# Residual held token-major: projections that end in it keep the activations stationary

## The chip, the cores and the metric

The program runs on one core of a Trainium2 chip. The metric is the device time of one execution in microseconds (us). An engine is named as the profile names it: PE is TensorE (its matmuls; PEld its weight loads), DVE is VectorE, ACT is ScalarE, POOL is GpSimd and SP is the engine that issues most DMAs. Each works through its own instructions in order and waits for the others through semaphores.

## The reference

Two layers are applied to x of 256 tokens by 2048 features, all in float32. Cut to what matters here:

```python
# first block
h = rms_norm(x, norm_mix_g)
proj = h @ w_in                                   # attention, recurrence, short convolution, gates
x = x + (g_a * y_a + g_b * y_b + g_c * y_c) @ w_out
h = rms_norm(x, norm_mlp_g)
x = x + jnp.square(jax.nn.relu(h @ w_mlp_up)) @ w_mlp_down      # 2048 -> 8192 -> 2048
x = rms_norm(x, final_g)
# second block
h = rmsnorm(x, g_mix_2) @ w_in_2                  # state space branch, sparse attention
x = x + jnp.concatenate([y_ssd, y_att], axis=-1) @ w_out_2
u = rmsnorm(x, g_mlp_2) @ w_up_2
return x + jnp.square(jax.nn.relu(u)) @ w_down_2
```

rms_norm(x, g) is x / sqrt(mean over features of x squared + 1e-6) * g. The x that goes from line to line is the residual.

## The kernel before, in words

**Jobs.** All large products are jobs of 512 output columns of a weight matrix. A job walks over the 2048 (or 1024) inputs in steps of 256, that is two blocks k of 128. For a step SP loads 256 x 512 weights into a tile `raw`; ACT rounds them to `hi` (a float32r value) and DVE computes the rest `lo = raw - hi`. Activations are split in the same way into an `Operand` of 16 blocks, each with a high and a low half of 256 tokens. A product is hi*hi + hi*lo + lo*hi, accumulated in PSUM (`products`).

**Two forms of a job.** Where the weights are stationary, each 128x128 piece of `hi` is loaded into PE and the 512 columns "high and low half" of the operand stream past it; each piece of `lo` sees the 256 columns of the high half. The output has features on the partitions and tokens along the row, its two partial sums side by side; `total` adds them (an ACT copy `cr`, a DVE add `tot`). A job has two outputs of 256 features, q = 0 and 1, each of two PSUM banks. In the other form, `tok=True`, 128 tokens of the operand are stationary and 512 columns of weights stream past them: hi*hi, hi*lo and lo*hi are each a matmul of 512 columns into the same place, and the output has tokens on the partitions. Before, this form serves for the values v of both attentions and for the last down-projection (f = 3 of the second block), whose result is stored to memory as it is.

**Residual.** `self.res` is four tiles, features on the partitions. `load_x` turns x with PE (`xT`), copies it by DVE to `xf` and writes that to memory as `xs`; the output projection loads it back. `residual` is the evacuation of jobs that end in the residual. It adds the job's result (in the down-projections scaled by a row `rrow`), and at the last addition it also makes the next operand (`split_scaled`) and sums squares over features (`squares`). `norm` in `output` and `between` fold these sums, reduce them over partitions with PE (`mean`), take the inverse square root in small DVE steps (`rsqrt`), and spread a column over a row with PE (`row`). `next_res` scales the residual for the second block and writes it to `xs`. `turn_res` turns the residual back (32 transposes, in the last up-projection) for the last jobs.

**What sets the order.** `stream` writes the instructions of all engines in program order; each engine then runs its own in that order. For each step it issues the loads 7 steps ahead, the split of weights 5 steps ahead, then the step's matmuls. Behind them `side.tick` lets short work of the branches (lanes) go on where a cost model says its inputs are ready, and `advance` takes each pending evacuation one `yield` further. At a job's last step its evacuation begins at once. Weight-stationary jobs do q = 0 of their first two steps before q = 1 of either. The output projection of the second block is cut in two halves over its inputs, so that it can begin while attention still runs.

**Jobs in order.** First block: 28 jobs of `w_in` with three branches between them, then the output projection (4 jobs, operand `mixop`), then for f = 0 to 3 four up-projections (operand `hm`) and four down-projections (operand `hid`, by `relu2`). Second block: jobs of `w_in_2` (operand `h`, side lanes beside them), the output projection in 8 halves (operand `ymix`), and again f = 0 to 3.

All instructions have line 104 in the profile, which is the helper that records them, so they are told apart by their tiles. Tiles are slots of 128 x 1024 float32, 43 in number, shared by weights, operands and residual.

Of the kernel before, what the change touches and what calls it, by code (L numbers as in the profile page):

```python
# [19 lines left out]
P = 128  # L20
T = 256
# [153 lines left out]
class Builder:  # L175
# [188 lines left out]

    def fold(self, acc):
        self.nc.vector.tensor_tensor(acc[:, 0, :], acc[:, 0, :], acc[:, 1, :], op=OP.add)
# [46 lines left out]
    def load_x(self, load):  # L413
# [5 lines left out]
        self.xs = self.dram.tile([P, 16, T], F32, name="xs")  # L419
        self.rstd, self.rstd_t = self.consts.tile([P, T], F32, name="rstd"), self.consts.tile([P, 2], F32, name="rstd_t")  # L420
        sums = self.consts.tile([P, 2, 4], F32, name="sums")
        xf = {}
# [6 lines left out]
        def turn(k):  # L429
            ps = self.side_ps(f"xT{k}").rearrange("p (k t) -> p k t", k=2)  # L430
            for i in range(2):
                for t in range(2):
                    nc.tensor.transpose(ps[:, i, t * P:(t + 1) * P],
                                        pieces[k // 4][:, t, (k % 4 + i) * P:(k % 4 + i + 1) * P], self.ident)
            if k % 4 == 0:
                xf[k // 4] = self.big(f"xf{k // 4}")
            nc.vector.tensor_copy(xf[k // 4][:, k % 4:k % 4 + 2, :], ps)

        def high(k):
            self.split_scaled_hi(self.h, k, xf[k // 4][:, k % 4:k % 4 + 2, :], g)  # L440
            if k % 4 == 2:
                nc.scalar.dma_start(self.xs[:, k - 2:k + 2, :], xf[k // 4])

        def low(k):
            self.split_scaled_lo(self.h, k, xf[k // 4][:, k % 4:k % 4 + 2, :], g)

        def norm():
            m = self.consts.tile([P, 2], F32, name="m1")
            nc.vector.tensor_reduce(m, sums, axis=AX.X, op=OP.add)
            nc.vector.tensor_scalar(m, m, 1.0 / D, None, op0=OP.mult)  # L450
# [309 lines left out]
    def first_block(self):  # L760
# [10 lines left out]
        w = lambda c: self.wload(w_in, c)  # L771
        before, between, load = self.load_x(w(3072))
# [79 lines left out]
        return jobs + self.output(d["w_out"][0], get("mixop"), "norm_mlp_g")  # L852
# [6 lines left out]
    def output(self, w, op, gvec, wait=None):  # L859

        def first():
            self.res = [self.big(f"res{i}") for i in range(4)]
            for i, r in enumerate(self.res):
                self.nc.gpsimd.dma_start(r, self.xs[:, 4 * i:4 * i + 4, :])
            self.acc = self.new_acc()
            self.hm = Operand(self, "hm")

        def norm():
            self.rt = self.consts.tile([P, 2], F32, tag="rt", name="rt")
            self.rrow = self.consts.tile([P, T], F32, tag="rrow", name="rrow")  # L870
            self.fold(self.acc)
            yield
            yield
            yield
            m = self.mean(self.acc[:, 0, :])
# [3 lines left out]
            yield  # L879
            yield  # L880
            self.row(self.rrow, self.rt)
        jobs = []
        for half in range(2 if wait else 1):
            last = half == 1 or not wait
            for j in range(4):
# [5 lines left out]
                def evac(q, ps, j=j, last=last):  # L891
                    more = dict(gvec=self.vec[gvec], op=lambda: self.hm, sq=((self.acc, None),)) if last else {}
                    return self.residual(j, **more)(q, ps)
                jobs.append(Job(16, self.wload(w, 512 * j), op, evac, before=before,
# [521 lines left out]
```

## Time and profile before

| | us |
|---|---|
| median of 3 runs | 2722.08 (2720.92 to 2723.45) |
| the profiled execution | 2721.87 |
| its span, first to last instruction | 2720.0 |
| PE busy in the span | 2702.6 |
| DVE busy | 1728.0 |
| ACT busy | 1281.0 |
| POOL busy | 44.4 |

Busy time counts from the start of an instruction to its end. Matmuls are pipelined, so one that takes 0.39 us may start 0.23 us behind the one before; the distance between starts tells what PE can do, the duration does not. Of the 512 MB that the DMA engines move, nearly all is weights, at a mean of 188 GB/s.

### The profile page before, as it was taken

To read this page: it belongs to the slowest core of one execution; us is meant where nothing else is said; L and a number is where in the kernel's file an instruction comes from. 1 tells how busy PE (TensorE), PEld (TensorE's weight loads), DVE (VectorE), ACT (ScalarE), POOL (GpSimd) and SP (SyncE) were. 2 spreads that over 40 slices of the span, in tenths; PEclk is the share of its full clock that TensorE was granted. 3 is DMA by queue.
4 is the path that set the end of the run, shared out by engine and by line. 5 is a ranking of instruction groups with operands and counts; after the bars stand their busy time and mean duration, and the time that the engine had idled before them with its cause. 6 is when DMAs were issued, how large, how long until landed. Compare 5 with 4: busy or idle time off the path is not lost.

```text
span 2720.0 us, 38654 instructions
## 1 busy us (share of the span) xinstructions
PE 2702.6 (99%) x15382; PEld 2344.9 (86%) x15382; DVE 1728.0 (64%) x2331; ACT 1281.0 (47%) x1705; POOL 44.4 (2%) x91
## 2 busy tenths in 40 slices
PE   8999999999999999999999999999999999999999
PEld 7888888888888888888888888788888888888887
DVE  7666655656576655556566679687785555655553
ACT  5645544434455444444444455455554344444442
POOL 3100000000000000000000000000000000000000
PEclk9999999999999999999999999999999999999999
DMA  8655565655665556556565557455565655655644
GB/s 300 179 185 159 188 197 191 197 181 184 201 224 193 178 178 204 177 191 195 180 210 180 190 159 231 133 183 188 174 189 180 200 179 179 207 175 190 188 150 166
DMA packets 268404, 512.33 MB, mean 188 GB/s; under 512 B 23034, under 2 KB 23298, under 8 KB 268224
## 3 DMA queue, kind: packets, MB, share of 16 engines
q1 hardware_dynamic: 263360, 496.30, 57.1%
q0 software_dynamic: 4256, 11.46, 1.4%
q8 instruction: 121, 1.98, 0.3%
q10 hardware_dynamic: 608, 2.11, 0.2%
q14 instruction: 59, 0.48, 0.1%
HBM read 503.29 MB, written 6.50 MB: 187 GB/s over the span
## 4 chain that ended last, share of the span: by engine, by line
PE 98%; DVE 1%; DMA 1%; ACT 0%; issue 0%; DVEq 0%; SPq 0%
PE ps L104 95%; PE ix L104 0%; PE sc L104 0%; PE pv L104 0%; DMA raw<-w_in 0%; PE lg L104 0%; PE xT L104 0%; PE ps_row L104 0%; PE py L104 0%; DVE lo L104 0%; PE pT L104 0%; PE hn L104 0%; DMA xt<-x 0%; ACT hi L104 0%; PE ps_mean L104 0%
## 5 line engine op out<-in xcount | busy, mean ns | idle before, releaser
L104 DVE TENSOR_TENSOR lo<-raw,hi 128x1024 fp32r<-128x1024 f32 (+1 forms) x944 | 1102.0, 1217 | 148.9 <-ACT hi L104 147.4
L104 ACT CAST hi<-raw 128x1024 fp32r<-128x1024 f32 (+1 forms) x944 | 926.1, 1043 | 71.0 <-DMA raw<-w_down 41.3
L104 PE MATMUL ps<-h,hi 128*128 128x512 f32 x2336 | 813.1, 396 | 3.8 <-DVE tot L104 2.0
L104 PE MATMUL ps<-hm,hi 128*128 128x512 f32 x2048 | 705.4, 395 | 0.0
L104 ACT COPY cr<-ps 128x512 f32<-128x512 f32 x241 | 141.2, 587 | 1097.2 <-PE ps L104 1097.2
L104 PE MATMUL ps<-h,lo 128*128 128x256 f32 x2336 | 634.7, 282 | 2.7 <-DVE lo L104 2.7
L104 DVE TENSOR_TENSOR tot<-ps,cr 128x512 f32<-128x512 f32 x230 | 158.4, 691 | 730.6 <-ACT cr L104 730.4
L104 PE MATMUL ps<-hid,hi 128*128 128x512 f32 x1792 | 615.1, 394 | 0.0
L104 PE MATMUL ps<-hm,lo 128*128 128x256 f32 x2048 | 548.6, 278 | 0.0
L104 PEld LDWEIGHTS ps<-h,hi 128*128 128x128 f32 x2336 | 430.6, 188 | 93.9 <-DVE tot L104 2.9
L104 PE MATMUL ps<-hid,lo 128*128 128x256 f32 x1792 | 478.5, 277 | 0.0
L104 PEld LDWEIGHTS ps<-h,lo 128*128 128x128 f32 x2336 | 440.4, 189 | 21.1 <-issue 3.4
L104 PEld LDWEIGHTS ps<-hm,hi 128*128 128x128 f32 x2048 | 376.2, 188 | 78.2
L104 PEld LDWEIGHTS ps<-hm,lo 128*128 128x128 f32 x2048 | 384.8, 188 | 11.3
L104 PEld LDWEIGHTS ps<-hid,hi 128*128 128x128 f32 x1792 | 328.9, 188 | 68.2
L104 PEld LDWEIGHTS ps<-hid,lo 128*128 128x128 f32 x1792 | 336.4, 188 | 9.9
L104 PE MATMUL ps<-ymix,hi 128*128 128x512 f32 x256 | 89.3, 397 | 0.0
L104 PE MATMUL ps<-mixop,hi 128*128 128x512 f32 x256 | 87.9, 394 | 0.0
L104 PE MATMUL ps<-hi,hid 128*128 128x512 f32 x256 | 79.0, 389 | 0.0
L104 PE MATMUL ps<-mixop,lo 128*128 128x256 f32 x256 | 68.3, 277 | 0.0
L104 PE MATMUL ps<-ymix,lo 128*128 128x256 f32 x256 | 67.3, 283 | 0.0
L104 PE MATMUL ps<-hi,h 128*128 128x512 f32 x192 | 61.6, 395 | 0.0
(304 smaller groups left out, 1785.8 us busy)
## 6 DMA issues: line engine op xcount, KB each, us to landing
raw<-w_in SPq DMA_DIRECT2D x312, 512.0 KB, 4.1
raw<-w_mlp_up SPq DMA_DIRECT2D x128, 512.0 KB, 4.1
raw<-w_mlp_down SPq DMA_DIRECT2D x128, 512.0 KB, 4.6
raw<-w_up SPq DMA_DIRECT2D x128, 512.0 KB, 4.2
raw<-w_down SPq DMA_DIRECT2D x128, 512.0 KB, 4.4
raw<-w_out SPq DMA_DIRECT2D x64, 512.0 KB, 4.5
raw<-w_attn_o SPq DMA_DIRECT2D x16, 512.0 KB, 4.4
raw<-w_lru_o SPq DMA_DIRECT2D x16, 512.0 KB, 4.3
```

The lines of the kernel that those rows point to most:

```text
L104: return f(out, *args, **kw)
```

## The change

The residual is held with tokens on the partitions, in four tiles of 2 x 512 (two halves of the tokens, 512 features). Both output projections and all down-projections take the form with the activations stationary, so that their result has the residual's layout and `residual` adds it from PSUM in one or two DVE instructions, with per-token factors as columns. Squares are summed along the row by ACT (`row_squares`), and DVE forms the mean from the sums (`row_mean`). The operands that are made from the residual (`hm` of both blocks, and `h` of the second block) are turned by PE in groups of four 128x128 transposes (`turn`, tiles `rT`) and split straight from PSUM. x is loaded for the residual as it lies in memory; `load_x` splits from PSUM as well. At the end of the first block, final_g, loaded as a row into two tiles `gain`, multiplies the residual. `turn_res`, `next_res` and the uses of `fold`, `mean` and `row` for the residual are gone.

```diff
+    def turn(self, name, src, k):
+        ps = self.side_ps(name).rearrange("p (k t) -> p k t", k=2)
+        for i in range(2):
+            for t in range(2):
+                self.nc.tensor.transpose(ps[:, i, t * P:(t + 1) * P],
+                                         src[:, t, (k % 4 + i) * P:(k % 4 + i + 1) * P], self.ident)
+        return ps
+
+    def row_squares(self, sums, j, src):
+        for t in range(2):
+            sq = self.tmp.tile([P, 512], F32, tag="sq", name="rsq")
+            self.nc.scalar.activation(sq, src[:, t, :], AF.Square, accum_out=sums[:, t, j:j + 1])
...
         def turn(k):
-            ps = self.side_ps(f"xT{k}").rearrange("p (k t) -> p k t", k=2)
...
-            nc.vector.tensor_copy(xf[k // 4][:, k % 4:k % 4 + 2, :], ps)
+            turned[k] = self.turn(f"xT{k}", pieces[k // 4], k)
...
-    def residual(self, j, scale=None, gvec=None, sq=(), op=None):
+    def residual(self, j, scale=None, keep=None, sums=None, gain=None, op=None, gvec=None):
...
-            t = self.total(ps)
-            yield
-            k = 4 * j + 2 * q
-            r = self.res[j][:, 2 * q:2 * q + 2, :]
-            if scale is not None:
-                nc.vector.tensor_tensor(t, t, self.pairwise(scale()), op=OP.mult)
-            nc.vector.tensor_tensor(r, r, t, op=OP.add)
-            if op is not None:
+            r = self.res[j]
+            for t in range(2):
+                if scale is not None:
+                    nc.vector.scalar_tensor_tensor(r[:, t, :], ps[:, t, :], scale()[:, t:t + 1], r[:, t, :],
+                                                   op0=OP.mult, op1=OP.add)
+                elif keep is not None:
+                    nc.vector.scalar_tensor_tensor(r[:, t, :], r[:, t, :], keep()[:, t:t + 1], ps[:, t, :],
+                                                   op0=OP.mult, op1=OP.add)
+            if scale is None and keep is None:
+                nc.vector.tensor_tensor(r, r, ps, op=OP.add)
+            yield
+            if op is None:
+                return
+            self.row_squares(sums()[0], j, r)
+            if gain:
+                g = gain()[j // 2][:, 512 * (j % 2):512 * (j % 2) + 512]
+                nc.vector.tensor_tensor(r, r, g[:, None, :].to_broadcast([P, 2, 512]), op=OP.mult)
                 yield
-                self.split_scaled(op(), k, r, gvec)
-            for acc, g in sq:
-                self.squares(acc, k, r, g)
+                self.row_squares(sums()[1], j, r)
+                nc.gpsimd.dma_start(self.xs[:, j], r)
+            for k in (4 * j, 4 * j + 2):
+                turned = self.turn(f"rT{k}", r, k)
+                self.split_scaled(op(), k, turned, gvec)
+                yield
...
-                jobs.append(Job(16, self.wload(w, 512 * j), op, evac, before=before,
+                jobs.append(Job(16, self.wload(w, 512 * j), op, evac, tok=True, before=before,
...
-                                tok=f == 3 and not last, after=then,
-                                before=(lambda i: self.side.drain("turn")) if f == 3 and not last else None))
+                                tok=True, after=after if (f, j) == (3, 3) else None,
+                                before=self.load_gain if last and (f, j) == (3, 0) else None))
...
+        self.row_mean(self.sums12[0], m1)
+        self.row_mean(self.sums12[1], m2)
```

How this moves instructions is seen at three places. A row is an engine's next instruction (tile written, tiles read, size, how many in a row). First PE, at the end of the first output projection (operand `mixop`, last job) and the start of the up-projection behind it (operand `hm`). Before:

```order
L104 MATMUL ps_1_7886<-mixop_7314,hi_7967 128x512
L104 MATMUL ps_1_7886<-mixop_7314,lo_7968 128x256
L104 MATMUL ps_1_7886<-mixop_7314,hi_7967 128x512
L104 MATMUL ps_0_8089<-hm_7505,hi_7989 128x512
L104 MATMUL ps_0_8089<-hm_7505,lo_7990 128x256 x2
L104 MATMUL ps_0_8089<-hm_7505,hi_7989 128x512 x2
L104 MATMUL ps_0_8089<-hm_7505,lo_7990 128x256 x2
L104 MATMUL ps_0_8089<-hm_7505,hi_7989 128x512
L104 MATMUL ps_0_8089<-hm_7511,lo_8012 128x256
```

With the change:

```order
L104 MATMUL ps_0_7759<-hi_7834,mixop_7301 128x512 x2
L104 MATMUL ps_0_7759<-lo_7835,mixop_7301 128x512
L104 MATMUL ps_0_7759<-hi_7834,mixop_7301 128x512
L104 MATMUL ps_0_7929<-hm_7441,hi_7852 128x512
L104 MATMUL ps_0_7929<-hm_7441,lo_7853 128x256 x2
L104 MATMUL ps_0_7929<-hm_7441,hi_7852 128x512 x2
L104 MATMUL ps_0_7929<-hm_7441,lo_7853 128x256 x2
L104 MATMUL ps_0_7929<-hm_7441,hi_7852 128x512
L104 MATMUL rT_7943<-ident,res_7253 128x128 x4
L104 MATMUL ps_0_7929<-hm_7469,lo_7871 128x256
```

The matmuls of the output projection are all 512 long, and four transposes of the residual's last tile stand behind the first four pairs of the next job. Behind the other jobs of such a projection they stand behind the 12 matmuls of the next token-major step; a second group follows a step later.

The same place on DVE (low parts `lo` of weights, the residual `res`, low halves of `hm`). Before:

```order
L104 TENSOR_TENSOR lo_8048<-raw_8009,hi_8047 128x1024
L104 TENSOR_TENSOR tot<-ps_0_7885,cr 128x512
L104 TENSOR_TENSOR tot<-ps_1_7886,cr 128x512
L104 TENSOR_TENSOR lo_8086<-raw_8031,hi_8085 128x1024
L104 TENSOR_TENSOR res_7273<-res_7273,tot 128x512 x2
L104 TENSOR_TENSOR lo_8104<-raw_8045,hi_8103 128x1024
L104 SCALAR_TENSOR_TENSOR hm_8115<-res_7273,vec_late_556,hm_8115 128x256 x2
L104 TENSOR_TENSOR acc<-acc,sq 128x512
```

With the change:

```order
L104 TENSOR_TENSOR lo_7907<-raw_7868,hi_7906 128x1024
L104 TENSOR_TENSOR res_7253<-res_7253,ps_0_7759 128x1024
L104 TENSOR_TENSOR lo_7926<-raw_7886,hi_7925 128x1024
L104 SCALAR_TENSOR_TENSOR hm_7948<-rT_7943,vec_late_538,hm_7948 128x256 x2
L104 TENSOR_TENSOR lo_7956<-raw_7904,hi_7955 128x1024
L104 SCALAR_TENSOR_TENSOR hm_7972<-rT_7967,vec_late_538,hm_7972 128x256 x2
```

One add takes the job's result from PSUM into the residual, with no low part between the two; the low halves of `hm` come from the turned tile.

At the end of the first block the residual is also multiplied by the gain. DVE there, with the change (`h` is the second block's operand):

```order
L104 SCALAR_TENSOR_TENSOR res_7253<-ps_0_13349,rt,res_7253 128x512 x2
L104 TENSOR_TENSOR lo_13524<-raw_13482,hi_13523 128x1024
L104 TENSOR_TENSOR res_7253<-res_7253,gain_12832 128x1024
L104 TENSOR_TENSOR lo_13545<-raw_13500,hi_13544 128x1024
L104 SCALAR_TENSOR_TENSOR h_13566<-rT_13561,vec_late_538,h_13566 128x256 x2
```

and PE in the first job of the second block, its second step and what follows:

```order
L104 MATMUL ps_0_13527<-h_13069,lo_13467 128x256
L104 MATMUL ps_0_13527<-h_13069,hi_13466 128x512
L104 MATMUL rT_13561<-ident,res_7253 128x128 x4
L104 MATMUL ps_1_13528<-h_13041,hi_13448 128x512
L104 MATMUL ps_1_13528<-h_13041,lo_13449 128x256 x2
```

Here the group stands behind two steps of q = 0, eight pairs; a low part of weights stands between the adds and the gain. Before, no transposes stood here.

## Rows read from the trace of the kernel before

**Rows 1.** The page: busy time, share and instructions; the chain that ended last.

```profile
PE 2702.6 (99%) x15382; PEld 2344.9 (86%) x15382; DVE 1728.0 (64%) x2331; ACT 1281.0 (47%) x1705; POOL 44.4 (2%) x91
...
PE 98%; DVE 1%; DMA 1%; ACT 0%; issue 0%; DVEq 0%; SPq 0%
```

**Rows 2.** Stretches: length; PE, PEld, DVE, ACT, POOL busy (instructions); clock, DMA share, GB/s.

```profile
886.40:976.20 89.80, 89.80 (x521) 78.59 (x520) 57.37 (x77) 41.22 (x52) 0.00 (x0) 1.00 0.57 175
...
1899.20:2000.10 100.90, 100.90 (x594) 88.78 (x593) 78.87 (x132) 59.77 (x107) 0.00 (x0) 1.00 0.54 178
...
2445.10:2533.90 88.80, 88.80 (x513) 77.65 (x512) 51.82 (x55) 36.93 (x42) 0.00 (x0) 1.00 0.60 201
2533.90:2627.50 93.60, 93.60 (x545) 81.62 (x544) 53.28 (x57) 43.17 (x54) 0.00 (x0) 1.00 0.58 181
2627.50:2714.80 87.30, 87.28 (x385) 71.89 (x383) 39.87 (x38) 30.18 (x31) 0.00 (x0) 1.00 0.41 144
```

**Rows 3.** Timeline, PE, last down-projection: start, length, engine, instruction, count.

```profile
2627.53 0.40 PE L104 MATMUL ps<-hi,hid 128*128 128x512 f32 x1
...
2714.39 0.39 PE L104 MATMUL ps<-hi,hid 128*128 128x512 f32 x1
```

**Rows 4.** Timeline, PE, the first transposes of turn_res.

```profile
2540.85 0.60 PE L104 MATMUL xT<-ident,res 128*128 128x128 f32 x4
2541.21 0.36 PE L104 MATMUL ps<-hm,lo 128*128 128x256 f32 x1
2541.41 0.39 PE L104 MATMUL ps<-hm,hi 128*128 128x512 f32 x1
```

**Rows 5.** Timeline, PE, three transposes in a token-major job of the first block.

```profile
181.86 0.49 PE L104 MATMUL pT<-ident,s 128*128 128x128 f32 x3
182.11 0.48 PE L104 MATMUL ps<-hi,h 128*128 128x512 f32 x1
182.43 0.39 PE L104 MATMUL ps<-lo,h 128*128 128x512 f32 x1
```

**Rows 6.** Timeline, PE, norm between the blocks; in brackets idle time and its releaser.

```profile
1615.88 0.95 PE L104 MATMUL ps_mean<-ones,acc 128*128 128x1 f32 x8
...
1622.17 0.40 PE L104 MATMUL ps<-h,hi 128*128 128x512 f32 x1
1623.10 0.68 PE L104 MATMUL ps_row<-ident,s_t 128*128 128x128 f32 x4 [0.53 <-DVE s_t L104]
...
1626.39 0.61 PE L104 MATMUL ps_row<-ident,r 128*128 128x128 f32 x4
```

**Rows 7.** Timeline, DVE, behind the last matmul of the program.

```profile
2714.82 1.41 DVE L104 SCALAR_TENSOR_TENSOR xt<-ps,rt,xt 128x512 f32<-128x512 f32 x2 [12.25 <-PE ps L104]
```

**Rows 8.** Groups by line and form: count, busy us, mean ns, idle before and releaser.

```profile
L104 DVE SCALAR_TENSOR_TENSOR xt<-ps,rt,xt 128x512 f32<-128x512 f32 x8 | 5.6, 746 | 30.5 <-PE ps L104 30.5
...
L104 DVE TENSOR_TENSOR ra<-ra,rw 128x2 f32<-128x2 f32 x24 | 3.9, 161 | 0.8
...
L104 DVE TENSOR_TENSOR u<-u,xc 128x1024 f32<-128x1024 f32 x2 | 2.4, 1224 | 0.1
...
L104 ACT ACTIVATE xsq<-xt 128x512 f32<-128x512 f32 x8 | 4.9, 618 | 0.0
L104 ACT ACTIVATION_READ_ACCUMULATOR xsq<-xt 128x1 f32 x8 | 1.5, 186 | 0.0
```

**Rows 9.** Timeline, PE, end of the last up-projection, 80 us behind the first transposes.

```profile
2621.64 0.40 PE L104 MATMUL ps<-hm,hi 128*128 128x512 f32 x1
...
2627.29 0.40 PE L104 MATMUL ps<-hm,hi 128*128 128x512 f32 x1
```

**Rows 10.** Timeline, all engines, the start.

```profile
6.61 0.69 DVE L104 COPY xf<-xT 128x512 f32<-128x512 f32 x1 [1.70 <-PE xT L104]
...
7.34 0.91 ACT L104 ACTIVATE h<-xf,vec_x 128x256 fp32r<-128x256 f32 x2 [4.75 <-DVE xf L104]
...
9.23 0.80 PE L104 MATMUL ps<-h,hi 128*128 128x512 f32 x1 [1.81 <-ACT hi L104]
```

More of the change, by code (lines that the diff above doesn't have):

```diff
@@ L850, in first_block, with output @@
                             before=before))
-        return jobs + self.output(d["w_out"][0], get("mixop"), "norm_mlp_g")
+        return jobs + self.output(d["w_out"][0], get("mixop"), lambda j: x[:, :, 512 * j:512 * (j + 1)], "norm_mlp_g")
     def new_acc(self):
         return self.tmp.tile([P, 2, T], F32, tag="acc", name="acc", bufs=2)
-    def output(self, w, op, gvec, wait=None):
+    def output(self, w, op, src, gvec, wait=None, keep=None):
         def first():
[L862 to L865, printed above, removed]
+            self.res = [self.slots.tile([P, 2, 512], F32, tag="slot", name=f"res{j}") for j in range(4)]
+            for j, r in enumerate(self.res):
+                self.nc.gpsimd.dma_start(r, src(j))
+            self.sums = self.consts.tile([P, 2, 4], F32, tag="sums", name="sums")
             self.hm = Operand(self, "hm")
@@ L869, in norm @@
             self.rt = self.consts.tile([P, 2], F32, tag="rt", name="rt")
[L870 to L875 removed]
+            m = self.consts.tile([P, 2], F32, tag="rm", name="rm")
+            self.row_mean(self.sums, m)
             yield
@@ L913, in feed_forward, with load_gain @@
                 if f < 3:
-                    evac = lambda q, ps, j=j: self.residual(j, scale=lambda: self.rrow)(q, ps)
+                    evac = lambda q, ps, j=j: self.residual(j, scale=lambda: self.rt)(q, ps)
                 elif last:
-                    evac = lambda q, ps, j=j: self.residual(j, scale=lambda: self.rrow, **last(j))(q, ps)
+                    evac = lambda q, ps, j=j: self.residual(j, scale=lambda: self.rt, **last(j))(q, ps)
                 else:
                     evac = lambda q, ps, j=j: self.store(j)(q, ps)
-                then = after if (f, j) == (3, 3) else None
-                if not last and (f, j) == (2, 3):
-                    then = lambda: self.side.add("turn", self.turn_res())
                 jobs.append(Job(16, self.wload(down[2048 * f:2048 * (f + 1)], 512 * j), lambda hid=hid: hid[0], evac,
-                                tok=f == 3 and not last, after=then,
-                                before=(lambda i: self.side.drain("turn")) if f == 3 and not last else None))
-        return jobs
+                                tok=True, after=after if (f, j) == (3, 3) else None,
+                                before=self.load_gain if last and (f, j) == (3, 0) else None))
+        return jobs
+    def load_gain(self, i):
+        if i:
+            return
+        g = self.d["final_g"]
+        self.gain = [self.slots.tile([P, 1024], F32, tag="slot", name=f"gain{n}") for n in range(2)]
+        for n, t in enumerate(self.gain):
+            self.nc.gpsimd.dma_start(t, bass.AP(tensor=g.tensor, offset=g.offset + 1024 * n, ap=[[0, P], [1, 1024]]))
     def first_end(self):
@@ L931, in last @@
         def last(j):
-            if not hasattr(self, "acc2"):
-                self.acc, self.acc2 = self.new_acc(), self.new_acc()
+            if not hasattr(self, "sums12"):
+                self.sums12 = [self.consts.tile([P, 2, 4], F32, name=f"sums{n}") for n in range(2)]
                 self.h = Operand(self, "h2")
-            return dict(gvec=self.fgg, op=lambda: self.h, sq=((self.acc, None), (self.acc2, V["final_g"])))
+                self.xs = self.dram.tile([P, 4, 2, 512], F32, name="xs")
+            return dict(gvec=V["g_mix_2"], op=lambda: self.h, sums=lambda: self.sums12, gain=lambda: self.gain)
         return last
@@ L1305, in wait @@
                 self.side.drain(*[f"att{n}" for n in range(4)]) if j == 0 else None
-        return [jobs[n] for n in ORDER.split()] + self.output(d["w_out_2"][0], lambda: st["ymix"], "g_mlp_2", wait)
-    def turn_res(self):
-        nc = self.nc
-        self.xt = [self.slots.tile([P, 2, 512], F32, tag="slot", name=f"xt{j}") for j in range(4)]
-        for j in range(4):
-            for t in range(2):
-                ps = self.side_ps("xT")
-                for i in range(4):
-                    nc.tensor.transpose(ps[:, i * P:(i + 1) * P], self.res[j][:, i, t * P:(t + 1) * P], self.ident)
-                nc.scalar.copy(self.xt[j][:, t, :], ps)
-                yield
+        return [jobs[n] for n in ORDER.split()] + self.output(d["w_out_2"][0], lambda: st["ymix"], lambda j: self.xs[:, j],
+                                                                 "g_mlp_2", wait, lambda: self.r1)
     def store(self, j):
```

64 lines of the change are left out of this document (17 added, 47 removed).

## The prediction

> **What bounds the kernel now.** The page is read first, and in it the busy times and the chain that ended last [rows 1]: TensorE (PE) has work for 2702.6 of 2720.0 us and carries 98% of the chain, while VectorE (DVE) is busy 64% and ScalarE (ACT) 47% of the time. So what a change does to the time is what it does to PE's stream of matmuls; work of DVE, ACT or the queues counts only where PE comes to wait for it. The second view is the table of stretches [rows 2], cut where the jobs change operand. A job is 512 output columns of a projection over 16 blocks of 128 inputs. Four jobs with the weights stationary are 512 matmuls (half of them 512 columns long, half 256) and take 88.80 us, 22.20 us a job, in all the down-projection stretches, of which one stands there. The last stretch holds the only down-projection that already has the activations stationary: four jobs in 384 matmuls, all 512 long. Its first and last matmul start at 2627.53 and 2714.39 [rows 3], 383 steps of 0.2268 us, so a job of 96 takes 21.77 us. The granted clock is 1.00 (the 2.4 GHz level) in both, and both stream 49152 columns a job. Both come out at 0.0134 us a matmul above the columns at that clock (a pair of 768 columns: 88.80/256 = 0.3469 against 0.3200; one of 512: 0.2268 against 0.2133). A job in the new form is shorter because it has 96 matmuls for 128.
>
> **The change part by part.** The sum is made against the profiled execution, 2721.87 us (span 2720.0 and 1.9 around it), 0.21 below the median of 2722.08.
>
> *Jobs turned round.* Both output projections (4 jobs each; the second is cut in 8 halves), the four down-projections of the first block (16) and three of the second (12) make 36 jobs. 36 x (22.20 - 21.77) = 15.5 us less. The Trainium skill (TensorE: Matmul & The Clock Gate, section "Wait — 56ns, not 53.3ns?") says that a warm matmul starts N / 2.4 GHz and about 2.5 ns behind the one before, the 2.5 ns fixed. By that a job goes from 20.80 to 20.72 us, an estimate, and the 36 jobs give 2.9 us. The trace has 13.4 ns where that page has 2.5, in both forms.
>
> *Operands transposed.* hm of each block and the second block's h are now made by turning the residual on PE: 3 operands x 8 groups of four 128x128 transposes = 24 groups. The trace has such groups in the stretch at 2533.90. Four start at 2540.85, the next matmul 0.36 us later at 2541.21, and that one holds 0.20 where 256 columns and 0.0134 make 0.12 [rows 4]: 0.44, say 0.45 a group among weight-stationary jobs. In a token-major job, three transposes push the next matmul from 181.86 to 182.11, and its 512 columns then take 0.32 instead of 0.227 [rows 5]; with a fourth at 0.11 that is 0.36 + 0.09, and I add 0.02 for the slightly longer steps behind it: 0.47. Of each operand's 8 groups 6 stand in the next token-major job and 2 in the first weight-stationary one (the order shows it): 18 x 0.47 + 6 x 0.45 = 11.2 us more. Bounds: 0.36 a group (8.6) and 0.60 (14.4), the latter being all that the 93.60 us stretch has over 88.80, by 8 groups.
>
> *Transposes that go.* turn_res goes with all of that excess: 93.60 - 88.80 = 4.8 us less [rows 2].
>
> *Sums over features.* The squares were folded on PE by ones and the row spread again by PE. Now the sums lie along a row of the tile, by ACT's accumulator, and the scale is a column. The two stretches with a norm (886.40, and a like one at 2000.1) take 89.80 for 88.80: 2.0 us less. Between the blocks eight small mean matmuls (0.95) and the row of r (four matmuls of 128 columns, 0.45 like a group) go, 1.4 us. PE also stood there for the row s_t: 0.93 from 1622.17 to 1623.10, where 0.23 is usual [rows 6]. In the order that row stood four pairs behind the first job's end and now stands eight pairs before it, at 21.8 us of the stage with the wait below. Its chain on DVE I have at 19.6: the last group is turned at 9.4; then two operands on ACT (1.0) and two low parts of h (1.0), two low parts of weights (1.9), and 32 small steps of 0.16 [rows 8] with a little between them. So the 0.7 goes too, 2.1 us in all; bounds 1.0 and 2.1, since a late weight in front of the chain would bring a wait back.
>
> *New waits.* A group of transposes stands in PE's stream, so all matmuls behind it wait if the residual is late. DVE starts 0.04 us after the last matmul of a job has landed, 0.20 after the next job's first may start [rows 3, 7], since it had waited there (12.25 us). In the output projections it then has one add of 128x1024; the row of that size takes 1.22 [rows 8], so the residual is there at 1.45. In a token-major job 12 matmuls, 2.72 us, lie in between: no wait for three of four. Behind the fourth comes a weight-stationary job, whose first step has only four pairs, 1.39: a wait of about 0.1, twice. At the end of the first block the residual takes two scaled adds (1.41 together, [rows 7]), then the gain: DVE has one low part ahead of it (1.22), and the gain may only overwrite what ACT has squared, two squares of 0.62 and 0.19 each [rows 8]. That makes 0.20 + 1.41 + 1.22 + 1.22 = 4.05, or 4.5 if the squares start behind both adds. In token-major jobs two steps, 5.44, lie between; before the fourth group only eight pairs, 2.78. The wait there is 1.3 to 1.7; I take 1.5, and 1.7 in all. Bounds 0 and 3.
>
> *Cadence after an interruption.* Behind the eight groups at 2533.90 the pairs ran at 0.353 (16 pairs from 2621.64 to 2627.29, [rows 9]) instead of 0.347, 0.41 us a job, until the token-major jobs began. The two first up-projections with new groups, 8 jobs, could do so: 0 to 3.3 us; I take 1.6.
>
> *Start.* x's transposes are no longer copied to SBUF by DVE. The copy (0.69, [rows 10]) stood ahead of ACT's h, which waited for it, and so ahead of the first matmul: 0.7 less, and perhaps as much again later in that first job; I take 1.0, bounds 0 and 1.6.
>
> *At nothing.* The evacuation loses ACT's copy and at least two of DVE's four to six passes a job; PE covered it and still does. POOL's four writes of the residual to memory now stand ahead of the memsets for the small projection, whose loads SP issues behind them: the last write can go at about 4.5 us of the second block, and those weights are used after 22 us, so some 10 us are in hand. The first residual comes from x, and final_g's two loads are issued a whole job, 21.8 us, ahead of their use.
>
> Sum: -15.5 + 11.2 - 4.8 - 2.0 - 2.1 + 1.7 + 1.6 - 1.0 = -10.9. From 2721.87 that is 2711.0, and as a median, 0.2 higher, **2711.2 us**.
>
> **The rivals.** *Slower: DVE comes late to every residual.* The place is DVE's queue at the ends of the 12 jobs whose residual is turned. It decides when the residual is later than 2.72 us (5.44 with the gain) behind the job's end. With two more low parts (2 x 1.22) in front, the output projections have it at 3.9: three waits of 1.2 and one of 2.5, 6.0 each. The first block's end has it at 6.5 to 6.9: three of about 1.3 and one of 3.9, 7.8. Together 19.8 in place of 1.7: 2711.2 + 18.1 = 2729.3. For it speaks the second output projection, where DVE is busy 78.87 of 100.90 us [rows 2]; against it that DVE sat idle ahead of the adds at the ends of before's token-major jobs, 30.5 us in four of them [rows 7, 8], and that its work per job falls.
>
> *Columns alone count.* If PE's time went by columns, 49152 in either form, the turned jobs would save nothing: 2711.2 + 15.5 = 2726.7, within the measurement. Rows 2 and 3 speak against it. With the 2.5 ns a matmul that the Trainium skill states (the page and section above) it would be nearly this case, 2723.8.
>
> *The slow cadence stays.* If pairs ran at 0.353 in all 32 up-projection jobs, it would cost 13.1 instead of 1.6: 2722.7. For it: [rows 9] lie 80 us behind the first group there. Against: the stretch at 886.40 has side matmuls in its first job too and only 1.0 over 88.80 [rows 2].
>
> That the change does not do what it says is excluded by the order.
>
> **How the numbers follow.** Forecast 0.78, with its own range 2706 to 2716.5 from the bounds (they do not all fall on one side); more than that, by shorter waits beside the side work, 0.03; columns 0.05; cadence 0.08, in part or whole; DVE late 0.06. The range is 2705 to 2720. A difference under 0.2% (5.4 us: 2716.6 to 2727.5) cannot be told from none. Faster 0.78 + 0.03 = 0.81, same 0.05 + 0.08 = 0.13, slower 0.06.
>
> **What would show it.** Right: four-job stretches of down-projection at about 87.1; 24 groups named rT with the next matmul 0.36 behind the first transpose; a wait of some 1.5 us at the first rT of the second block's first job and nearly none elsewhere; no groups in the last up-projection, 88.8. Wrong: token-major stretches at 88.8, groups over 0.6, waits before rT in token-major jobs, or pairs at 0.353 throughout.

## The result and the profile after

The changed kernel takes 2707.43 us (median of 4 runs, 2706.96 to 2707.89), the kernel before 2721.83 (4 runs, 2720.92 to 2723.45): a ratio of 0.9946, 95% interval 0.9929 to 0.9964, 14.4 us less. The forecast was 2711.2, range 2705 to 2720: faster as predicted and in the main by the mechanism predicted, and 3.8 us shorter than the sum had.

The page of the changed kernel, answering [rows 1]: PE still has work for all but 15.5 us of the span, with 1116 matmuls fewer, and DVE, which was never the bound, lost 113 us.

```profile
span 2705.7 us, 36217 instructions
...
PE 2690.2 (99%) x14266; PEld 2296.7 (85%) x14266; DVE 1614.7 (60%) x2135; ACT 1246.6 (46%) x1641; POOL 44.2 (2%) x92
...
PE 98%; DVE 1%; ACT 1%; issue 0%; DMA 0%; DVEq 0%
```

The table of stretches of the changed kernel, cut at the same places of the program (length; PE, PEld, DVE, ACT, POOL busy; clock, DMA share, GB/s): first output projection, first up-projection, first down-projection, the first block's last down-projection, the second block's first projections, second output projection, last up-projection, last down-projection.

```profile
795.70:885.70 90.00, 90.00 (x410) 74.47 (x409) 50.35 (x54) 42.13 (x60) 0.00 (x0) 1.00 0.59 200
885.70:975.50 89.80, 89.80 (x521) 78.39 (x520) 54.87 (x72) 39.73 (x52) 0.00 (x0) 1.00 0.54 171
975.50:1062.50 87.00, 87.00 (x385) 72.06 (x384) 43.13 (x42) 40.88 (x41) 0.00 (x0) 1.00 0.63 210
1503.00:1593.00 90.00, 90.00 (x410) 74.46 (x409) 52.34 (x57) 46.15 (x72) 1.60 (x3) 1.00 0.62 196
1593.00:1869.30 276.30, 274.68 (x1594) 231.14 (x1593) 211.11 (x468) 140.14 (x210) 8.32 (x18) 1.00 0.53 166
1894.20:1996.50 102.30, 102.30 (x490) 85.25 (x488) 67.44 (x109) 53.39 (x99) 0.00 (x0) 1.00 0.54 179
2525.10:2613.90 88.80, 88.80 (x514) 77.61 (x513) 51.02 (x54) 32.43 (x39) 0.00 (x0) 1.00 0.58 186
2613.90:2701.00 87.10, 87.10 (x385) 71.88 (x383) 39.85 (x38) 30.17 (x31) 0.00 (x0) 1.00 0.41 144
```

Two stretches of the kernel before that [rows 2] did not show, the first output projection and the second block's first projections:

```profile
797.60:886.40 88.80, 88.80 (x513) 77.64 (x512) 57.41 (x69) 44.55 (x60) 0.00 (x0) 1.00 0.61 198
1597.80:1874.20 276.40, 275.33 (x1597) 231.73 (x1596) 220.94 (x491) 141.51 (x210) 9.27 (x17) 1.00 0.56 173
```

Six down-projections go from 88.80 to 87.0 (384 matmuls for 512) and the last up-projection from 93.60 to 88.80. An output projection is no shorter than before: 90.0 for 88.8, 102.3 for 100.9, since six groups of transposes now stand in it, and the first block's last down-projection takes 90.0 for the same reason. The first up-projections stay at 89.80.

PE's timeline of the changed kernel (start, length, instruction; in brackets idle time and its releaser): a group in the first output projection; the second group of the first up-projection; the wait in the second block's first job; the row s_t.

```profile
820.18 0.60 PE L104 MATMUL rT<-ident,res 128*128 128x128 f32 x4
820.54 0.47 PE L104 MATMUL ps<-hi,mixop 128*128 128x512 f32 x1
820.85 0.39 PE L104 MATMUL ps<-lo,mixop 128*128 128x512 f32 x1
...
889.03 0.60 PE L104 MATMUL rT<-ident,res 128*128 128x128 f32 x4
889.38 0.47 PE L104 MATMUL ps<-hm,hi 128*128 128x512 f32 x1
889.70 0.40 PE L104 MATMUL ps<-hm,lo 128*128 128x256 f32 x2
...
1595.51 0.40 PE L104 MATMUL ps<-h,hi 128*128 128x512 f32 x1
1596.99 0.63 PE L104 MATMUL rT<-ident,res 128*128 128x128 f32 x4 [1.08 <-DVE res L104]
...
1614.33 0.39 PE L104 MATMUL ps<-h,hi 128*128 128x512 f32 x1
1614.56 0.61 PE L104 MATMUL ps_row<-ident,s_t 128*128 128x128 f32 x4
```

The next matmul starts 0.36 behind the first transpose and holds 0.31 where 0.227 is usual, as in [rows 5]. The one wait that can be seen is 1596.99 - 1595.51 - 0.23 = 1.25. The row s_t, which waited in [rows 6], starts 0.23 behind the matmul ahead of it: no wait. DVE's chain in front of the one wait, and ACT's first square, in the same kernel:

```profile
1593.17 1.41 DVE L104 SCALAR_TENSOR_TENSOR res<-ps,rt,res 128x512 f32<-128x512 f32 x2 [6.06 <-PE ps L104]
1594.49 1.21 DVE L104 TENSOR_TENSOR lo<-raw,hi 128x1024 fp32r<-128x1024 f32 x1
1595.62 1.22 DVE L104 TENSOR_TENSOR res<-res,gain 128x1024 f32<-128x1024 f32 x1
...
1594.01 0.63 ACT L104 ACTIVATE rsq<-res 128x512 f32<-128x512 f32 x1 [7.96 <-DVE res L104]
```

Two scaled adds, one low part of the weights, the gain: the order that the prediction gave. The gain is done at 1596.84, 3.9 behind the next job's first matmul (1592.96), where it had 4.05, and PE starts the group 0.15 later. The last row is the first of ACT's squares.

And the start of the changed kernel, answering [rows 10]:

```profile
6.64 0.84 ACT L104 ACTIVATE h<-xT,vec_x 128x256 fp32r<-128x256 f32 x2 [0.24 <-PE xT L104]
...
8.46 0.80 PE L104 MATMUL ps<-h,hi 128*128 128x512 f32 x1 [1.01 <-ACT hi L104]
```

The first matmul stands at 8.46 for 9.23, and the first output projection starts at 795.70 for 797.60.

### The profile page after: what moved, and what is told of

It is laid out like the page before. It is cut to its first block, busy times and chain, and to the rows that moved or that the text cites. A ratio compares the mean times of both kernels' runs of the same rounds, so it can differ in the third digit from the quotient of the medians.

```text
span 2705.7 us, 36217 instructions
## 1 busy us (share of the span) xinstructions
PE 2690.2 (99%) x14266; PEld 2296.7 (85%) x14266; DVE 1614.7 (60%) x2135; ACT 1246.6 (46%) x1641; POOL 44.2 (2%) x92
## 4 chain that ended last, share of the span: by engine, by line
PE 98%; DVE 1%; ACT 1%; issue 0%; DMA 0%; DVEq 0%
PE ps L104 95%; PE ix L104 1%; PE rT L104 0%; PE sc L104 0%; PE pv L104 0%; PE lg L104 0%; DVE lo L104 0%; PE py L104 0%; PE pT L104 0%; ACT hi L104 0%; PE hn L104 0%; DMA xt<-x 0%; PE xT L104 0%; PE ps_row L104 0%; DVE res L104 0%
## 5 line engine op out<-in xcount | busy, mean ns | idle before, releaser
L104 PE MATMUL ps<-hi,hid 128*128 128x512 f32 x2048 | 633.4, 389 | 0.0
L104 PEld LDWEIGHTS ps<-hi,hid 128*128 128x128 f32 x2048 | 384.5, 188 | 79.4
L104 ACT COPY cr<-ps 128x512 f32<-128x512 f32 x161 | 94.3, 587 | 740.0 <-PE ps L104 739.9
L104 PE MATMUL ps<-lo,hid 128*128 128x512 f32 x1024 | 398.4, 389 | 0.0
L104 PEld LDWEIGHTS ps<-hm,lo 128*128 128x128 f32 x2048 | 384.5, 188 | 11.2
L104 DVE TENSOR_TENSOR tot<-ps,cr 128x512 f32<-128x512 f32 x150 | 103.0, 689 | 486.9 <-ACT cr L104 486.8
L104 DVE SCALAR_TENSOR_TENSOR res<-ps,rt,res 128x512 f32<-128x512 f32 x64 | 45.1, 746 | 318.9 <-PE ps L104 318.9
L104 PEld LDWEIGHTS ps<-lo,hid 128*128 128x128 f32 x1024 | 192.3, 188 | 39.8
L104 PE MATMUL ps<-hi,ymix 128*128 128x512 f32 x256 | 84.6, 399 | 0.0
L104 PE MATMUL ps<-hi,mixop 128*128 128x512 f32 x256 | 80.7, 392 | 0.0
L104 PEld LDWEIGHTS ps<-hi,mixop 128*128 128x128 f32 x256 | 48.1, 188 | 9.9
```

Of the source, the lines that this page charges most:

```text
L104: return f(out, *args, **kw)
```

## The experiments

All start from the changed kernel. Times are medians; the kernel before ran beside them at 2722.3 to 2722.6.

**As many matmuls as before, same columns.** The edit, in all down-projections:

```diff
-nc.tensor.matmul(o, op.lo(k)[:, t], hi[:, kk, :], ...)
+for n in range(2):
+    nc.tensor.matmul(o[:, n*T:(n+1)*T], op.lo(k)[:, t], hi[:, kk, n*T:(n+1)*T], ...)
```

> The changed kernel, but in the 32 down-projection jobs (all token-major) the third matmul of each block, the one with the low part of the activations, is cut into two of 256 columns. A job then has 128 matmuls, as many as a weight-stationary one, and streams the same 49152 columns. Theory (a matmul costs its columns and 0.0134 us): a stretch of four such jobs goes from 87.05 to 87.05 + 128 x 0.0134 = 88.77 us, the program from 2707.4 to 2721.1 us (+13.7). Rival (columns alone count): 87.05 and 2707.4, no change. By the 2.5 ns a matmul that the Trainium skill states (TensorE: Matmul & The Clock Gate, section 'Wait - 56ns, not 53.3ns?') a stretch would take 87.4 and the program 2710.0.

Measured: 2725.24 us (10 runs; ratio to before 1.0009, 1.0000 to 1.0019). Two stretches of the cut kernel:

```profile
975.90:1065.10 89.20, 89.20 (x514) 77.81 (x513) 43.32 (x42) 40.77 (x41) 0.00 (x0) 1.00 0.63 206
2451.60:2540.80 89.20, 89.20 (x514) 77.83 (x513) 43.33 (x42) 40.79 (x41) 0.00 (x0) 1.00 0.60 206
```

With 128 matmuls a job the whole gain is gone: 17.8 more than the changed kernel (13.7 expected). The price is (89.20 - 87.05)/128 = 0.0168 us a matmul, a little over the 0.0134 of the theory. "Columns alone count" is refuted. The 2.5 ns of the Trainium skill (TensorE: Matmul & The Clock Gate, section "Wait — 56ns, not 53.3ns?") is not what these operands pay, which is 13.4 to 16.8 ns. Every matmul here has a weight load of its own (514 beside 513 in the rows), so the price is that of a matmul with its load; the two were not told apart.

**Half of the transposes.**

```diff
 for k in (4 * j, 4 * j + 2):
-    turned = self.turn(f"rT{k}", r, k)
+    if k == 4 * j:
+        turned = self.turn(f"rT{k}", r, k)
```

> The changed kernel with every second group of transposes of the residual left out: 12 groups in place of 24. The operand blocks of the group that is left out are made from the transposes of the group before it, so half of hm and of the second block's h hold the wrong features; all else is computed as before. Price of a group: a token-major stretch with three groups in place of six should go from 90.0 to 87.05 + 3 x 0.49 = 88.5 us; 12 groups at 0.47 and 0.45 make -5.6, so 2701.8 us (0.36 a group: 2703.1, 0.60: 2700.2). Second question, the slow cadence. Theory A: pairs run at 0.353 behind an interruption whose next matmul is one of 256 columns in the middle of a PSUM half, and at 0.347 again behind one that stands ahead of a half's first matmul. The first up-projection of each block then ends its transposes in the middle of a half: 89.8 - 0.45 + some 240 pairs x 0.0062 = 90.8 us, twice, and the total is 2704.8. Theory B (the cadence does not depend on the place): 89.3 us and 2701.8.

Measured: 2705.46 us (2704.8 by theory A, 2701.8 by B). The first output projection, the first up-projection and the second block's first up-projection of this kernel:

```profile
796.20:884.70 88.50, 88.50 (x398) 73.25 (x397) 49.83 (x54) 42.13 (x60) 0.00 (x0) 1.00 0.60 203
884.70:975.60 90.90, 90.90 (x517) 78.81 (x516) 54.88 (x72) 39.86 (x52) 0.00 (x0) 1.00 0.54 169
...
1993.70:2084.60 90.90, 90.90 (x517) 78.73 (x516) 54.89 (x72) 39.83 (x52) 0.00 (x0) 1.00 0.53 170
```

Three groups less save 1.5 in a token-major stretch: 0.49 each, as expected. But the up-projections get slower with one group in place of two, 90.9 for 89.8, as theory A says: the group that is left stands in the middle of a PSUM half. (A half is one of a job's two outputs q. Its first matmul has 512 columns; a pair in its middle begins with the one of 256.)

**Idle transposes at chosen places.**

```diff
+ps = self.side_ps("poke")
+for i in range(n):
+    self.nc.tensor.transpose(ps[:, i*P:(i+1)*P], self.ident, self.ident)
```

> The changed kernel with idle transposes of the identity (nobody reads them) put into the six up-projections that follow another one in their block (88.8 us each without): one group of 4 in the middle of a PSUM half of the first job, next matmul 256 columns (first block, second up-projection); a group of 4 ahead of a half's first matmul, 512 columns (third); one of each, the second two jobs later (fourth); 3 transposes, then 1, in the middle of a half (second block, second and third); 4 between the two matmuls of a pair, next matmul 512 (fourth). Theory A (place sets the cadence of the pairs that follow, 0.353 behind a 256, 0.347 ahead of a half's first): 88.8 + 0.43 + 228 pairs x 0.0062 = 90.6; 89.3; 0.9 + 112 x 0.0062: 90.4; 90.5; 90.4; the last 89.3 if only the next matmul's columns matter, 90.6 if the half's start does. Theory B (only the transposes cost): 89.25, 89.25, 89.7, 89.15, 88.95, 89.25.

Measured: 2715.05 us (one run). The six up-projections, in the order of the expectation:

```profile
1061.90:1152.40 90.50, 90.50 (x518) 78.78 (x517) 51.05 (x54) 32.45 (x39) 0.00 (x0) 1.00 0.54 170
1239.50:1328.70 89.20, 89.20 (x517) 78.02 (x516) 51.04 (x54) 32.43 (x39) 0.00 (x0) 1.00 0.54 173
1415.80:1506.60 90.80, 90.80 (x521) 79.12 (x520) 51.05 (x54) 32.44 (x39) 1.11 (x2) 1.00 0.59 192
2177.60:2268.00 90.40, 90.40 (x517) 78.63 (x516) 51.04 (x54) 32.44 (x39) 0.00 (x0) 1.00 0.53 171
2355.10:2445.20 90.10, 90.10 (x515) 78.41 (x514) 51.05 (x54) 32.43 (x39) 0.00 (x0) 1.00 0.54 171
2532.30:2621.50 89.20, 89.20 (x517) 78.07 (x516) 51.04 (x54) 32.43 (x39) 0.00 (x0) 1.00 0.58 184
```

A group costs 0.4 alone (89.20 for 88.80); behind one, three or four transposes in the middle of a half the pairs also go to 0.353 and add 1.2 or so to the stretch. Ahead of 512 columns they do not. Theory A holds to 0.3 but for the third row (90.8, expected 90.4): a second group, ahead of a half, did not bring the pairs back.

**VectorE late, first try.** Two adds of 128x1024 into an unread tile, ahead of the residual's add.

```diff
+for n in range(2 if op is not None else 0):
+    ...                                    # the tile late
+    nc.vector.tensor_tensor(late, r, r, op=OP.add)
```

> The changed kernel with two more VectorE adds of 128x1024 (about 1.22 us each, into a tile that nobody reads) ahead of the residual in the 12 jobs whose residual is turned. It makes the rival 'DVE late to every residual' come true by 2.44 us. If the room behind a job's end is 2.72 us in the output projections and 5.44 us at the first block's end, as the prediction has it, the residual comes at 3.9 and 6.5 to 6.9: waits of 1.2 in three jobs and 2.5 in the fourth of each output projection, 1.0 to 1.4 in three and 3.7 in the fourth at the first block's end, together some 18 us more: 2725 us, the three token-major stretches at 93 to 94 where 90 was (second output projection 106). Rival: VectorE has more room than that and most of the 2.44 us is hidden: below 2715 us.

Measured: 2709.04 us. The try was badly built for its purpose: the adds need nothing of PE, so DVE ran them while it waited for the job's last matmul. Only at the end of the second output projection were they late, in DVE's timeline of this kernel:

```profile
1996.80 2.48 DVE L104 TENSOR_TENSOR late<-res 128x1024 f32<-128x1024 f32 x2
1999.38 1.22 DVE L104 TENSOR_TENSOR res<-res,ps 128x1024 f32<-128x1024 f32 x1
```

There the up-projection behind it grew by 1.2. So the rival was mispriced: low parts of the weights that stand in front of the add should be able to run ahead in the same way (argued from this; not tried with low parts).

**VectorE late, on the chain.**

```diff
+for n in range(2 if op is not None else 0):
+    nc.vector.tensor_tensor(r, r, r, op=OP.max)
```

> The changed kernel with two VectorE operations of 128x1024 (max of the residual with itself, 1.22 us each, the values stay) behind the residual's add in the 12 jobs whose residual is turned, so that the residual itself comes 2.44 us later; in the earlier try the two stood ahead of the add and could run while VectorE waited for PE. With a room of 2.72 us (5.44 at the first block's end) the residual is at 3.9 (6.4 there): waits of 1.2 in three jobs and 2.4 more in the fourth of each output projection, 1.0 in three and 2.4 more in the fourth at the first block's end: 12.0 + 5.4 = 17.4 us more, 2724.8 us, hence no gain over the kernel before. Rival (room enough, or the waits overlap with other idle time): below 2715 us.

Measured: 2735.30 us, 27.9 more. In its trace, PE's waits for the residual (us in total, times, longest); PE's timeline at a token-major job, at the first up-projection and at the second block's first job; and stretches (clock: third number from the end), three around the wait in the first up-projection, one behind the longest wait, and 78 us of the first up-projection of each block, well behind the waits.

```profile
PE rT L104 <- DVE res L104: 20.0, 12, 4.0
```

```profile
820.88 0.66 PE L104 MATMUL rT<-ident,res 128*128 128x128 f32 x4 [1.11 <-DVE res L104]
...
893.23 0.63 PE L104 MATMUL rT<-ident,res 128*128 128x128 f32 x4 [2.53 <-DVE res L104]
...
1612.00 0.88 PE L104 MATMUL rT<-ident,res 128*128 128x128 f32 x3 [4.02 <-DVE res L104]
```

```profile
890.00:893.00 3.00, 0.70 (x5) 0.34 (x3) 2.93 (x3) 0.00 (x0) 0.00 (x0) 1.00 0.56 175
893.00:897.00 4.00, 3.77 (x17) 3.33 (x18) 2.96 (x5) 2.99 (x7) 0.00 (x0) 0.61 0.38 112
...
901.00:905.00 4.00, 4.00 (x25) 3.52 (x24) 3.58 (x15) 2.79 (x3) 0.00 (x0) 1.00 0.31 85
...
1612.00:1616.00 4.00, 4.00 (x14) 3.61 (x15) 2.94 (x4) 2.90 (x7) 1.96 (x8) 0.50 0.58 172
...
905.00:983.00 78.00, 78.00 (x452) 68.18 (x451) 44.27 (x48) 30.32 (x37) 0.00 (x0) 1.00 0.53 172
2035.00:2113.00 78.00, 78.00 (x443) 67.68 (x443) 42.51 (x46) 30.31 (x37) 0.00 (x0) 1.00 0.52 169
```

Twelve waits where they were expected, 20.0 us of idle time. From start to start, as the 1.25 above was taken, they make 22.0 us, 20.5 more than in the changed kernel (17.4 expected): 1.3 to 1.4 in the output projections (1.2 expected), 1.4 to 1.5 at the first block's end (1.0), and 2.6, 2.6 and 2.9 more in the three fourth ones (2.4). So the room behind a job is as the prediction had it to 0.2 us, at the first block's end to 0.5, and a chain of DVE that is 2.44 longer takes the whole gain away.

The other 7 us come behind the three long waits (1.6, 2.5 and 3.1 us). After PE had stood for 2.53 us the granted clock averaged 0.61 over the next 4 us, between its two levels, and that up-projection took 94.0 for 89.85. Behind the wait of 4.02 it was 0.50, the lower level (1.2 GHz), for 4 us; behind the other of 2.53 it averaged 0.66 over 5 us from 2023. Of the last 3.1 us about 1 is the slow cadence. The two up-projections have the same code and their groups at the same places, yet the first ran on at 0.347 (452 matmuls in 78 us) and the second at 0.353 (443). Theory A has no reason for that.

**The copy at the start put back.**

```diff
-turned[k] = self.turn(f"xT{k}", pieces[k // 4], k)
+ps = self.turn(f"xT{k}", pieces[k // 4], k)
...
+turned[k] = xf[k // 4][:, k % 4:k % 4 + 2, :]
+nc.vector.tensor_copy(turned[k], ps)
```

> The changed kernel with VectorE's copy of x's transposes to SBUF put back at the start (but not the writes of x to memory). The prediction priced the copy at 1.0 us, 0.7 of it ahead of the first matmul; the stretch up to the first output projection is 1.9 us shorter in the changed kernel. If the copy is all of it, that stretch is 1.9 us longer again and the program takes 2709.3 us; if the prediction's 1.0 was right and the rest came from the four writes of 512 KB that went, 2708.4; if only the writes mattered, 2707.4.

Measured: 2709.41 us, 2.0 more, as expected if the copy is all of it. The trace says less. First a wait of PE in the kernel before; then, in this kernel, PE's first matmul and the same wait:

```profile
33.50 0.36 PE L104 MATMUL ps<-h,lo 128*128 128x256 f32 x1 [0.60 <-DVE lo L104]
...
9.12 0.79 PE L104 MATMUL ps<-h,hi 128*128 128x512 f32 x1 [1.81 <-ACT hi L104]
...
33.42 0.36 PE L104 MATMUL ps<-h,lo 128*128 128x256 f32 x1 [0.62 <-DVE lo L104]
```

The first matmul is at 9.12 again, and the wait at 33.5, which the changed kernel does not have, is back: 0.7 and, from start to start, 0.9. The first output projection starts at 797.0, 1.3 later than in the changed kernel. In the other kernels without the copy and with the same order up to there, that point lies between 795.1 and 796.6, so a single trace gives this term to 0.8 only. The second block's projections, whose code is the same, took 276.7 for 276.3. So the copy costs some 1.6 us by its own waits; that it makes all of the 1.9 is not shown.

**Both groups at one place.**

```diff
+if j == 3:
+    yield
-for k in (4 * j, 4 * j + 2):
-    turned = self.turn(f"rT{k}", r, k)
-    self.split_scaled(op(), k, turned, gvec)
-    yield
+turned = [(k, self.turn(f"rT{k}", r, k)) for k in (4 * j, 4 * j + 2)]
+for k, ps in turned:
+    self.split_scaled(op(), k, ps, gvec)
+yield
```

> The changed kernel with both groups of a job's residual turned at one place (eight transposes in a row), and, for the fourth residual of each operand, one step later, ahead of the first matmul of a PSUM half. Theory (a residual that is late costs PE the whole wait; a group costs 0.49 us, of which some 0.05 is saved where it stands behind another): the wait of 1.25 us in the second block's first job and the two of about 0.15 go, 12 joints save 0.05 each: -2.2, 2705.2 us, the token-major stretches at 89.8 for 90.0, the first up-projections at 89.5 to 89.6. Rival: what waited there is only moved (eight transposes need two side banks, and ACT and VectorE must make four blocks at once): 2707.4, with waits before the second rT of a pair.

Measured: 2705.06 us (4 runs, 2704.85 to 2705.80; ratio to before 0.9937, 0.9920 to 0.9955), 2.4 under the changed kernel: the fastest version here. PE at the second block's start, and the stretch of those projections:

```profile
1599.94 1.04 PE L104 MATMUL rT<-ident,res 128*128 128x128 f32 x8
```

```profile
1593.00:1868.00 275.00, 274.46 (x1593) 231.20 (x1592) 211.07 (x468) 140.01 (x210) 8.27 (x18) 1.00 0.54 167
```

No idle time ahead of the transposes, and 1.3 off the stretch, with as many slow pairs in it as in the changed kernel (256 and 259 with more than 0.349 from start to start): the wait was a real cost and is not merely moved. The first output projection and both first up-projections take 89.7 (89.8 and 89.5 to 89.6 expected).

**The order of the pair.** Two attempts to use the cadence: 512 columns first in all pairs, and only in the first pair behind an interruption.

```diff
-if a: hi (512); lo (256); if not a: hi (512)      # in short: the matmuls of a pair in order
+hi (512); lo (256)
```

> The changed kernel with one order of matmuls in all weight-stationary jobs: the one of 512 columns (high part of the weights) first, then the one of 256, in every pair, where before only a half's first pair had it so and the other pairs had the 256 first. So an interruption at a step's end is always followed by 512 columns, and a half's start no longer turns the order round. Theory A (the slow cadence comes of an interruption that is followed by 256 columns, and sets in at the next half's start): no pairs at 0.353 are left. The pairs slower than 0.349 and not beside an interruption are 593 in the trace of the changed kernel, with an excess of 4.9 us: 2702.5 us. Theory B (it is the interruption itself): no change, 2707.4. Third case: 512 first is the slower order throughout, 0.353 in all pairs: about 20 us more, 2727.

Measured: 2731.55 us (10 runs, one of them 2720.84): the third case, but the same program once ran 10.7 us faster, which no case explains. The second up-projection of this kernel, with nothing in its way, runs at the slow cadence from end to end:

```profile
1074.40:1164.90 90.50, 90.50 (x514) 78.41 (x514) 51.04 (x54) 32.42 (x39) 0.00 (x0) 1.00 0.53 170
```

```diff
-if a:
+if a or broken and m == kk == 0:      # broken: PE did something else since the last step
```

> The changed kernel, where the first pair of matmuls behind any interruption of a weight-stationary job (transposes, norm matmuls, attention) is issued with the 512 columns first and then goes on as at a half's start (512, 256, 256, 512, ...); all else keeps its order, unlike the try with one order throughout (which ran at 0.353 nearly everywhere, and at 2720.8 in one of ten runs). Theory (an interruption ahead of 512 columns leaves the pairs fast, as the third and the last up-projection of the try with idle transposes showed): the 593 slow pairs go, -4.9: 2702.5 us; the second block's projections at 274 us for 276.3. Rival (the place among the step's matmuls does not matter there, or a doubled 512 costs as much): 2707.4.

Measured: 2708.61 us. The same edit together with both groups at one place:

> Both edits in one kernel: the two groups of a residual at one place and one step later for the fourth (2705.06 by itself), and the first pair behind an interruption with its 512 columns first. If the two add up: 2705.1 - 4.6 (the excess of the 567 slow pairs in that kernel's trace) = 2700.5 us; if the order of the first pair does nothing: 2705.1.

Measured: 2705.95 us. Neither gains (1.2 and 0.9 us more than without the edit). With the edit alone 360 of 630 pairs in the second block's projections were slower than 0.349, for 259 in the changed kernel, and the stretch took 277.2 for 276.3. So the columns of the next matmul do not decide. The place of an interruption does not do so alone either: with the copy put back or with the idle transposes, where the code of these projections is that of the changed kernel, 295 and 310 pairs were slow there, and with VectorE late on the chain the same places gave 0.347 once and 0.353 once. What decides is open.

## Why the prediction came out as it did

*Jobs turned round*: -15.5 predicted; 9 times (88.80 - 87.05) = -15.8 (87.05 is the mean of the six stretches by their starts). Right, and the cut matmuls show that the number of matmuls, each with its weight load, is enough for it at equal columns.

*Operands transposed*: +11.2. Six groups make (90.0 - 87.05)/6 = 0.49 each in token-major jobs; 0.35 + 0.09 = 0.44 in the others: 18 x 0.49 + 6 x 0.44 = 11.5. Right, with half of the transposes as the check.

*Transposes that go*: -4.8, and -4.8 came. The idle transposes give a price to what it was: eight groups at 0.44 are 3.5, and some 200 pairs at the 0.353 of [rows 9] make another 1.2.

*Sums over features*: -2.0 in the two stretches with a norm. They are 89.80 again, which is this gain against two groups (0.9) and the wait of 0.1 in each; it was not measured apart. *Between the blocks*: -2.1, with 0.9 for two groups and 1.25 for the wait, leaves 0.05; measured -0.1, in a stretch that differs by 0.6 between kernels with the same code there. Its parts were not measured apart either; the row s_t did stand without a wait.

*New waits*: 1.7 predicted; 1.25 and twice about 0.1 (at the first group of both first up-projections, by the distances between starts), so 1.5. Right in place and chain; the squares began behind the first add (1594.01, while DVE's adds ran to 1594.58), so the lower of the two values given held.

*Cadence after an interruption*: +1.6 predicted, 0 measured: the two first up-projections are at 89.85 by their starts, and two groups and the wait make up all that they have over 88.80. This step failed. It took the 0.353 of [rows 9] as a possible follower of any group. Half the transposes and the idle ones show that place matters: pairs went slow behind a group in the middle of a PSUM half, and stayed fast where it stood ahead of a half or of 512 columns. In both first up-projections a group ahead of a half follows the one in the middle. But place does not settle it, as the kernel with VectorE late on the chain shows, so why the term came out at the lower end of its bounds is open. The 89.80 of the norm stretches in [rows 2] pointed that way: they had side matmuls too.

*Start*: -1.0 predicted, -1.9 between the two traces. A mis-sized term. The 0.7 ahead of the first matmul was right (9.23 to 8.46). Behind it the prediction had 0.3; the wait at 33.50, which comes and goes with the copy, was worth 0.9. A wait at 41.61 for a low part of the weights is also shorter, 1.04 for 1.53, with the copy put back too, so that part is not the copy's; its cause was not looked for. The remaining -0.3 lies within the scatter of 0.8.

A further 0.6 lies behind the last matmul, in the stores (end of the span less start of the last matmul: 5.6 before, 5.0 after), where the same work is done in the same order; it was not pursued. The sum, with the two terms that were not measured apart (-2.0 and -2.1) as predicted: -15.8 + 11.5 - 4.8 - 2.0 - 2.1 + 1.5 - 1.9 - 0.6 = -14.2, where the spans differ by 14.3. So of the 3.3 that the sum was short, 1.6 is cadence, 0.9 start, 0.6 the end, and what is left the rest. All three err to the same side, so they add up, and the bounds had room for it. The other 0.5 of the 3.8 is what lies between the spans and the medians.

*The rivals.* Columns alone: refuted. Slow cadence in all up-projections: 88.8 in each but the two first. DVE late to every residual: did not happen, and its price was wrong both ways: work in front of the add costs nothing while DVE is idle, and work behind it cost 27.9 where the waits make 20.5, since behind the long ones the clock was lower as well.

## What to carry to other kernels

Where PE is the bound, count matmuls (with their weight loads) as well as columns, from a stretch of your own trace: here 0.013 to 0.017 us each, at equal columns, was worth more than all transposes that the other form needs. What must be made between two matmuls on PE belongs where its operand is surely ready, in one piece, a step late rather than a step early; check how much room the feeding engine has behind the job's end, by delaying what lies on the chain and not what lies in front of it.

## What the runs showed of the hardware that was not expected

The pairs of 512 and 256 columns have two cadences at full granted clock, 0.347 and 0.353 us, and may keep either for 80 us. The place of an interruption bears on it (90.1 to 90.5 against 89.2 for like groups) but does not decide: two stretches of one execution, with the same code and groups at the same places, ran one at each. One program with another order of the pair ran in 2731.55 us nine times out of ten, within 1.3 us, and in 2720.84 once. And single idle times of PE of 2.53 and 4.02 us were each followed by a lower granted clock for some microseconds (0.61 and 0.50 over 4 us), while behind the one of 1.08 us in the changed kernel the clock stayed at 1.00 and the pairs ran on at 0.347.
